# Expert groups of the two smallest counts in 32 places and four column tiles, in a two-layer mixture-of-experts trunk

## The chip, the cores and the metric

The kernel runs on one core of a Trainium2 chip, as one launch. The metric is the device time of that launch in microseconds (us), as the median of several runs. The engines are PE (TensorE matmul; its weight loads are listed as PEld), DVE (VectorE), ACT (ScalarE), POOL (GpSimd) and SP (SyncE, which here issues the weight transfers); 16 DMA engines move the data.

## What is computed

Two layers, each an attention-like mixer followed by a mixture of experts, over 512 tokens of width 1024. The change touches only the second half of a layer. Cut to that:

```python
def route(h, router_w, router_b):                     # 8 groups of 4 experts
    scores = jax.nn.sigmoid((h @ router_w).astype(jnp.float32))
    biased = scores + router_b.astype(jnp.float32)
    grp = biased.reshape(t, N_GROUPS, EXPERTS_PER_GROUP)
    group_score = jnp.sum(lax.top_k(grp, GROUP_SCORE_K)[0], axis=-1)
    g_sel = jnp.argmax(group_score, axis=-1)          # one group for each token
    in_group = (jnp.arange(N_EXPERTS) // EXPERTS_PER_GROUP)[None, :] == g_sel[:, None]
    _, idx = lax.top_k(jnp.where(in_group, biased, -jnp.inf), TOP_K)   # two experts of it
    w = jnp.take_along_axis(scores, idx, axis=-1)
    return idx, w / jnp.sum(w, axis=-1, keepdims=True)
...
    u = jax.nn.silu(xb @ w_gate[e]) * (xb @ w_up[e])  # 1024 -> 512
    y = (u @ w_down[e]) * gts[:, None]                # 512 -> 1024
...
    x = x + gt2 * y
```

A token goes to one group. With the reference's inputs the groups hold, sorted by count, 115, 96, 85, 71, 54, 46, 31 and 14 tokens in layer 0 and 108, 105, 94, 64, 50, 41, 30 and 20 in layer 1.

## The kernel before, in words

In each layer the kernel counts the tokens of each group, ranks the groups by count and gives each rank a fixed number of places: `CAPS` (line 31) is 128 for ranks 0 to 3 and 64 for ranks 4 to 7, 768 `PLACES` in all. A 0/1 matrix `Pt` gathers the normalized tokens into `hs`, whose columns are the places (L1370). All four experts of a group run on all places of the group; the gate weight of a place is zero where a token did not choose the expert. Tokens beyond a rank's places would be worked off by a loop behind `tc.If(nov > 0)` (L1686), which reads the group's weights again.

An expert is three matrices, each fetched as two transfers of 1 MB by SP (`fetch`, L1447) into one of eight raw buffers (tag `R8`: two in `ring`, four in `wm`, two in `late`). A transfer is issued as soon as the buffer's last user is done, so up to eight run ahead. Each transfer is used as two halves ("pieces"; `pieces` is asked for pieces up to four ahead of the one in use).

- A **wide** expert (rank 0 to 3) has each piece split into two parts by ACT and DVE (`split`) and runs three matmuls for each product (`three`): 24 matmuls of 512 columns for each of gate (`g`), up (`u`) and down (`y`).
- A **narrow** expert (rank 4 to 7) uses the raw fp32 weights as the moving operand and its 64 places as the stationary one; `halved` runs two matmuls side by side, one for each half of the columns, into the output partitions 0 to 63 and 64 to 127 (two column tiles). An fp32 matmul is two records in the trace.

`WHERE` (line 35) sets the order: **round** w (0 to 3) alternates the four experts of rank w with the four of rank w + 4; the last round ends with two wide experts and then two narrow ones. Within that order PE runs, for each expert e: gate of e + 1 (with the transposes of e, `turn`, in its midst), down of e, up of e + 1. When a group's fourth expert is done, its sum `ya` is multiplied with `gt2` and added back to the tokens (`combine`): it is cut into steps that are taken after each piece of the next experts. `combine_last` does the same for rank 7 at the end of the layer, with nothing beside it; in layer 0 it also makes the squares that the next layer's norm needs, in layer 1 it stores the result.

MoE-stage instructions of PE, DVE, ACT and POOL inside the expert loop keep their written order (`_Pinned`, whose line 122 stands in the trace for all of them). The next layer's first weights (`early`) are requested by SP right after the last expert's.

Of the kernel before, what the change touches and what calls it, by code (L numbers as in the profile page):

```python
# [139 lines left out]
def hybrid_trunk(ctx: ExitStack, tc: tile.TileContext, x, c, positions, w_mod, b_mod, norm1_g, norm2_g, w_in,  # L140
# [228 lines left out]
    for l in range(depth):  # L369
        first = l == 0  # L370
        with ExitStack() as ps:
# [919 lines left out]
            nth, rk, aw, cap, over, slot = [pt_([128, NT]) for _ in range(6)]  # L1291
# [4 lines left out]
            V.tensor_scalar(cap, rk, NWIDE - 0.5, CAPS[-1] - CAPS[0], op0=OP.is_gt, op1=OP.mult)  # L1296
            V.tensor_scalar(aw, rk, float(NWIDE), 0.0, op0=OP.subtract, op1=OP.max)
            V.tensor_scalar(cap, cap, float(CAPS[0]), None, op0=OP.add)
            V.scalar_tensor_tensor(aw, aw, CAPS[-1] / CAPS[0] - 1.0, rk, op0=OP.mult, op1=OP.add)
# [49 lines left out]
            def pre_done():  # L1349
# [7 lines left out]
                for n in range(2):  # L1357
                    A.dma_start(after["gt2h"][64 * n:64 * n + 64], bcast(mods[l, 5 * D + 512 * n:5 * D + 512 * n + 512], 512, 64))
# [134 lines left out]
            def up_part(src, e, gacc):  # L1493
                r, j = where[e]
                w = 512 if r < NWIDE else 256
# [5 lines left out]
                u_ = wm.tile([128, FE], tag="eu")[:, 0:w]  # L1501
                for q in range(w // 256):
# [5 lines left out]
            def turn(u_, e):  # L1508
# [7 lines left out]
                else:  # L1516
                    for k in range(2):
                        T.transpose(b[:, k], u_[:, k * 128:(k + 1) * 128], ident)
                    uT = wm.tile([128, 2, 128], tag="euT64")
                    A.copy(uT, b[:, 0:2])  # L1520
                return uT

            def down_part(src, e, uT, ya, amid=None):
                r, j = where[e]
                for k in range(4):
# [5 lines left out]
                    else:  # L1531
                        halved(ya[:, 0], uT[:, k % 2, 64 * (k // 2):64 * (k // 2) + 64], hl, 0, D, start, stop)
# [4 lines left out]
            def gain_y(ya, n, yf, wide_):  # L1537
                V.tensor_mul(yf, ya[:, n], after["gt2b"][:, n * 512:(n + 1) * 512] if wide_ else after["gt2h"])
                return yf

            def gated(ya, n, wide_):
                return parts(gain_y(ya, n, after["pool"].tile([128, 512], tag="eyf"), wide_))
# [253 lines left out]
```

## Time and profile before

| | us |
|---|---|
| median of 3 runs (1832.09 to 1835.33) | 1832.76 |
| the profiled execution | 1833.86 |
| its span, first to last instruction | 1832.1 |
| PE busy in the span | 1751.1 (96%) |
| DVE, ACT, POOL busy | 1113.6, 795.5, 88.9 |
| mean granted clock of PE | 0.98 of 2.4 GHz |
| read from HBM | 501.73 MB |

The span has two expert stages, one in each layer: about 449 to 964 us in layer 0 and 1312 to 1826 us in layer 1. In the rows, a busy share of PE says that a matmul was in flight, not that the array was full. "DMA share" is the mean busy share of the 16 DMA engines; where it is 1.0, they had a packet in hand all the time.

### The profile page before, as it was taken

What the parts mean: (1) busy time and instruction counts of PE and PEld (TensorE: products, weight loads), DVE (VectorE), ACT (ScalarE), POOL (GpSimd) and SP (SyncE); (2) the same over time, 40 slices, a digit from 0 to 9 for tenths busy, and PEclk for the clock granted to TensorE, in tenths of its full rate; (3) what the DMA queues carried; (4) which work ended last, traced back from release to release, by engine and by line L of the source; (5) the groups of instructions that cost most, each with busy time, mean ns of one, the idle gap of its engine ahead of it and who ended that gap; (6) DMA issues with size and microseconds to landing.
All of it is one profiled execution on the core that took longest, in us unless ns stands there. A gap on an engine that the chain in (4) does not pass through costs nothing. (4 is left out here: it accounts for less than half of the span.)

```text
span 1832.1 us, 28257 instructions
## 1 busy us (share of the span) xinstructions
PE 1751.1 (96%) x10891; PEld 1252.5 (68%) x10892; DVE 1113.6 (61%) x2004; ACT 795.5 (43%) x1215; POOL 88.9 (5%) x136
## 2 busy tenths in 40 slices
PE   5999999988999999999998999997999999999997
PEld 3866767777665666665748887986866666566673
DVE  4646564366548557566655778647555746756664
ACT  3344442354434443444523554445444344444450
POOL 1010000021000000000000110102000000000000
PEclk9999999998999999999998999998999999999998
DMA  9565547426999999999964211131899999999994
GB/s 329 159 220 181 176 154 227 161 97 267 368 421 374 396 422 365 413 422 355 423 249 141 70 47 47 47 131 47 322 381 421 364 411 422 360 414 416 360 421 180
DMA packets 115617, 512.11 MB, mean 280 GB/s; under 512 B 14978, under 2 KB 42896, under 8 KB 66320
## 3 DMA queue, kind: packets, MB, share of 16 engines
q1 hardware_dynamic: 111952, 504.93, 70.8%
q0 software_dynamic: 1072, 3.32, 0.5%
q10 hardware_dynamic: 2448, 1.94, 0.5%
q8 instruction: 89, 1.46, 0.3%
q14 instruction: 56, 0.46, 0.1%
HBM read 501.73 MB, written 8.42 MB: 278 GB/s over the span
## 5 line engine op out<-in xcount | busy, mean ns | idle before, releaser
L122 DVE TENSOR_TENSOR H<-R,H 128x1024 fp32r<-128x1024 f32 x368 | 431.2, 1219 | 97.6 <-ACT H L122 97.2
L122 ACT CAST H<-R 128x1024 fp32r<-128x1024 f32 x368 | 364.0, 1048 | 45.0 <-DMA R<-in_w_down_dram 27.5
L579 PEld LDWEIGHTS a<-H,u 128*128 128x128 f32 x1728 | 216.5, 190 | 45.0 <-issue 42.0
L579 PE MATMUL a<-H,u 128*128 128x256 f32 x1728 | 245.8, 291 | 0.0
L122 PE MATMUL y<-H,euT 128*128 128x512 f32 x768 | 188.6, 400 | 1.5 <-DVE euT L122 1.5
L122 PE MATMUL g<-H,exT 128*128 128x512 f32 x720 | 183.8, 402 | 0.0
L122 PE MATMUL u<-H,exT 128*128 128x512 f32 x720 | 177.0, 400 | 0.0
L122 PEld LDWEIGHTS y<-H,euT 128*128 128x128 f32 x768 | 141.6, 188 | 46.8 <-ACT H L122 9.2
L122 DVE SCALAR_TENSOR_TENSOR eu<-u,u,es 128x256 f32<-128x256 f32 x92 | 56.9, 672 | 191.5 <-PE u L122 191.5
L122 PEld LDWEIGHTS u<-H,exT 128*128 128x128 f32 x720 | 132.7, 188 | 54.1 <-issue 22.5
L122 PEld LDWEIGHTS g<-H,exT 128*128 128x128 f32 x720 | 131.4, 188 | 36.1 <-issue 8.5
L122 PE MATMUL g<-R,u 128*64 128x256 f32 x1024 | 126.9, 387 | 0.0
L122 PE MATMUL y<-R,euT 128*64 128x512 f32 x512 | 121.3, 602 | 1.1 <-ACT euT L122 1.1
L122 PE MATMUL u<-R,u 128*64 128x256 f32 x1024 | 118.9, 383 | 0.0
L122 DVE TENSOR_TENSOR u<-u,x 128x512 f32<-128x512 f32 x128 | 84.2, 682 | 45.7 <-PE x L122 45.5
L122 ACT COPY euT<-x 128x256 f32<-128x256 f32 x32 | 11.9, 372 | 211.8 <-PE x L122 191.2
L122 PEld LDWEIGHTS u<-R,u 128*64 128x64 f32 x1024 | 70.3, 137 | 45.2 <-issue 13.8
L122 PEld LDWEIGHTS g<-R,u 128*64 128x64 f32 x1024 | 67.0, 136 | 47.7 <-issue 20.6
L122 PE MATMUL x<-eyh,ePT 128*128 128x512 f32 (+1 forms) x256 | 75.5, 464 | 11.1 <-DVE u L122 7.5
L122 ACT CAST euT<-x 128x512 fp32r<-128x512 f32 x32 | 18.7, 584 | 151.5 <-PE x L122 151.5
L122 PEld LDWEIGHTS y<-R,euT 128*64 128x64 f32 x512 | 32.3, 136 | 63.7 <-issue 52.5
L122 PEld LDWEIGHTS x<-eyh,ePT 128*128 128x128 f32 (+1 forms) x256 | 34.0, 194 | 53.2 <-DVE u L122 33.0
(597 smaller groups left out, 2271.7 us busy)
## 6 DMA issues: line engine op xcount, KB each, us to landing
R<-in_w_gate_dram SPq DMA_DIRECT2D x128, 1024.0 KB
R<-in_w_up_dram SPq DMA_DIRECT2D x128, 1024.0 KB
R<-in_w_down_dram SPq DMA_DIRECT2D x128, 1024.0 KB
M<-in_w_mod_dram SPq DMA_DIRECT2D x80, 512.0 KB
R<-in_w_in_dram SPq DMA_DIRECT2D x20, 1024.0 KB
slab<-in_w_mod_dram SPq DMA_DIRECT2D x16, 512.0 KB
R<-in_w_in_dram SPq DMA_DIRECT2D x24, 256.0 KB
R<-in_w_out_dram SPq DMA_DIRECT2D x4, 1024.0 KB
```

The costliest lines, as they stand in the source:

```text
L122: return self.tc.keep_in_program_order(f(*args, **kw))
L579: T.matmul(acc[i // 2][:, i % 2], a[q][:, k, tk], hl[:, w, k], start=(i % 2 == 0 and q == 0 and k == 0 and n3 == 0), stop=(i % 2 == 1 and ...
```

## The change

Ranks 6 and 7 get 32 places instead of 64; ranks 0 to 5 keep theirs. `PLACES` becomes 736. For a rank of 32 places `halved` runs four matmuls side by side, each on a quarter of the columns, into the output partitions 0 to 31, 32 to 63, 64 to 95 and 96 to 127. For gate and up a quarter is every second column of one half (`wq`), so that one transposition instead of two turns the result. The sum `ya` of such a rank stands in 128 partitions by 256 columns; adding it back takes four quarter matmul groups for each of the four token tiles, in two rounds, instead of two half groups in one round. `gt2q` is a third copy of the output gain, loaded by four small transfers on ACT's queue. Two DVE instructions of 128x4 are added in the routing. The transfers of weights, their order, the buffers and the experts' order stay as they are.

```diff
-CAPS = (128,) * NWIDE + (64,) * (NG - NWIDE)
-OFFS = tuple(sum(CAPS[:r]) for r in range(NG))
-PLACES = sum(CAPS)
+CAPS = (128,) * NWIDE + (64,) * (NG - NWIDE - 2) + (32,) * 2
+OFFS = tuple(128 * min(r, NWIDE) + 64 * max(r - NWIDE, 0) for r in range(NG))
+PLACES = OFFS[-1] + CAPS[-1]
...
+            V.tensor_scalar(least, rk, NG - 2.5, CAPS[-1] - CAPS[NWIDE], op0=OP.is_gt, op1=OP.mult)
+            V.tensor_add(cap, cap, least)
...
-                for n in range(2):
-                    A.dma_start(after["gt2h"][64 * n:64 * n + 64], bcast(mods[l, 5 * D + 512 * n:5 * D + 512 * n + 512], 512, 64))
+                after["gt2q"] = wn.tile([128, 256])
+                for name, c in (("gt2h", 64), ("gt2q", 32)):
+                    w = D * c // 128
+                    for n in range(128 // c):
+                        o = 5 * D + w * n
+                        A.dma_start(after[name][c * n:c * (n + 1)], bcast(mods[l, o:o + w], w, c))
...
-            def halved(out, a, raw, c0, n, start, stop):
+            def halved(out, a, cap, columns, start, stop):
 
-                n //= 2
-                for h in range(2):
-                    T.matmul(out[64 * h:64 * h + 64, 0:n], a, raw[:, c0 + h * n:c0 + (h + 1) * n], start=start, stop=stop)
+                for h, w in enumerate(columns):
+                    T.matmul(out[cap * h:cap * (h + 1), 0:w.shape[-1]], a, w, start=start, stop=stop)
...
-                            halved(acc, hs[:, 2 * p + k, OFFS[r]:OFFS[r] + 64], hl, k * 512, 512, start, stop)
+                            w, cap = hl[:, k * 512:(k + 1) * 512], CAPS[r]
+                            wq = w.rearrange("p (q t k) -> p q k t", q=2, k=2)
+                            halved(acc, hs[:, 2 * p + k, OFFS[r]:OFFS[r] + cap], cap, [w[:, 0:256], w[:, 256:512]] if cap == 64 else
+                                   [wq[:, h // 2, h % 2] for h in range(4)], start, stop)
...
+                if w == 128:
+                    V.scalar_tensor_tensor(u_, acc[:, 0:w], gcs[:, r, j:j + 1], s, op0=OP.mult, op1=OP.mult)
...
-                        halved(ya[:, 0], uT[:, k % 2, 64 * (k // 2):64 * (k // 2) + 64], hl, 0, D, start, stop)
+                        cap, w = CAPS[r], D * CAPS[r] // 128
+                        a = uT[:, k % 2, 64 * (k // 2):64 * (k // 2) + 64] if cap == 64 else uT[:, 0, 32 * k:32 * k + 32]
+                        halved(ya[:, 0], a, cap, [hl[:, h * w:(h + 1) * w] for h in range(128 // cap)], start, stop)
...
-                if len(yhs) == 2:
+                w = min(512, D * cap // 128)
+                if cap == 128:
                     bs = [(n, pbank("x", 3), slice(0, 128), yhs[n]) for n in ns]
                 else:
-                    bs = [(n, pbank("x", 3), slice(64 * n, 64 * n + 64), yhs[0]) for n in ns]
+                    bs = [(n, pbank("x", 3)[:, 0:w], slice(cap * n, cap * n + cap), yhs[0]) for n in ns]
...
+            def rounds(r):
+
+                return {128: ((0,), (1,)), 64: ((0, 1),), 32: ((0, 2), (1, 3))}[CAPS[r]]
...
                 for i in range(NT):
-                    add(PT, yhs, (0, 1), i)
+                    for ns in rounds(r):
+                        add(PT, yhs, ns, i, CAPS[r])
```

On PE, in round 2 of layer 0, this stands between the up of a wide expert of rank 2 and the next one (`g`, `u`, `y` are gate, up and down; `R` is a raw buffer, `H` a split one; `eu` is transposed into `x`). Before:

```order
L122 MATMUL g_6687<-R_1241_6656,u_817_4391 64x256 x8
L122 MATMUL x_6704<-u_1_63,eu_6684 128x128 x4
L122 MATMUL g_6687<-R_1242_6670,u_817_4391 64x256 x8
L122 MATMUL y_6528<-H_1246_6690,euT_6709 128x512 x6
...
L122 MATMUL u_6758<-R_1253_6728,u_817_4391 64x256 x8
...
L122 MATMUL x_6808<-u_1_63,eu_6791 128x128 x2
...
L122 MATMUL y_1232_6628<-R_1265_6794,euT_1267_6811 64x512 x4
```

And now:

```order
L122 MATMUL g_6738<-R_1243_6707,u_818_4394 32x128 x16
L122 MATMUL x_6763<-u_1_63,eu_6735 128x128 x4
L122 MATMUL g_6738<-R_1244_6721,u_818_4394 32x128 x16
L122 MATMUL y_6556<-H_1248_6741,euT_6768 128x512 x6
...
L122 MATMUL u_6825<-R_1255_6795,u_818_4394 32x128 x16
...
L122 MATMUL x_6891<-u_1_63,eu_6874 128x128
...
L122 MATMUL y_1234_6671<-R_1267_6877,euT_1269_6893 32x256 x8
```

Nothing has changed places; each transfer of 1 MB is now used by twice as many matmuls of half the columns and half the outputs, and the narrow expert has one transpose instead of two.

On DVE, at the end of layer 0, `combine_last` stands between the last expert and the next layer's norm (`es` is the sum times the gain, `eyh` its split, `u_679` the tokens; L501 splits the next layer's early weights). Before:

```order
L122 TENSOR_TENSOR es_8123<-y_1403_7514,u_874_4751 128x512
L501 TENSOR_TENSOR H_1644_8638<-R_1537_8184,H_1644_8638 128x768
L122 TENSOR_TENSOR eyh_8125<-es_8123,eyh_8125 128x512
L501 TENSOR_TENSOR H_1647_8686<-R_1537_8184,H_1647_8686 128x768
L122 TENSOR_TENSOR u_679_3783<-u_679_3783,x_8128 128x512
L122 TENSOR_TENSOR u_679_3783<-u_679_3783,x_8129 128x512
...
L501 TENSOR_TENSOR H_1651_8738<-R_1538_8188,H_1651_8738 128x768
```

And now:

```order
L122 TENSOR_TENSOR es_8479<-y_1413_7745,u_876_4759 128x256
L122 TENSOR_TENSOR eyh_8481<-es_8479,eyh_8481 128x256
L122 TENSOR_TENSOR u_679_3783<-u_679_3783,x_8484 128x256
L122 TENSOR_TENSOR u_679_3783<-u_679_3783,x_8485 128x256
L501 TENSOR_TENSOR H_1662_9026<-R_1555_8572,H_1662_9026 128x768
L122 TENSOR_TENSOR u_679_3783<-u_679_3783,x_8492 128x256
L122 TENSOR_TENSOR u_679_3783<-u_679_3783,x_8493 128x256
L501 TENSOR_TENSOR H_1665_9074<-R_1555_8572,H_1665_9074 128x768
L122 TENSOR_TENSOR u_679_3783<-u_679_3783,x_8504 128x256
L122 TENSOR_TENSOR u_679_3783<-u_679_3783,x_8505 128x256
L501 TENSOR_TENSOR H_1669_9126<-R_1556_8576,H_1669_9126 128x768
```

The 8 additions of 512 columns have become 16 of 256; the early weights' splits stood before and behind the additions, and now all three stand among them.

## Rows read from the trace of the kernel before

**Rows 1.** The page's DMA issues: weight transfers of the experts, KB each.

```profile
R<-in_w_gate_dram SPq DMA_DIRECT2D x128, 1024.0 KB
```

**Rows 2.** Windows: us, busy PE PEld DVE ACT POOL, clock, DMA share, GB/s.

```profile
521.07:550.17 29.10, 29.10 (x159) 19.28 (x158) 16.36 (x16) 11.41 (x14) 0.00 (x0) 1.00 1.01 423
691.00:721.00 30.00, 28.73 (x140) 16.58 (x136) 23.27 (x34) 10.89 (x14) 0.00 (x0) 1.00 0.92 362
721.00:751.00 30.00, 30.00 (x164) 20.03 (x163) 17.52 (x18) 14.08 (x19) 0.00 (x0) 1.00 0.97 380
```

**Rows 3.** PE in order of time: start, us, matmuls; one undisturbed pair, then two starts.

```profile
521.07 1.95 PE L122 MATMUL g<-R,u 128*64 128x256 f32 x16
522.94 0.66 PE L122 MATMUL x<-u,eu 128*128 128x128 f32 x4
523.53 1.95 PE L122 MATMUL g<-R,u 128*64 128x256 f32 x16
525.41 5.84 PE L122 MATMUL y<-H,euT 128*128 128x512 f32 x24
531.17 3.67 PE L122 MATMUL u<-R,u 128*64 128x256 f32 x32
534.78 3.07 PE L122 MATMUL g<-H,exT 128*128 128x512 f32 x12
540.79 3.65 PE L122 MATMUL y<-R,euT 128*64 128x512 f32 x16
544.38 5.86 PE L122 MATMUL u<-H,exT 128*128 128x512 f32 x24
...
676.89 1.95 PE L122 MATMUL g<-R,u 128*64 128x256 f32 x16
745.39 1.95 PE L122 MATMUL g<-R,u 128*64 128x256 f32 x16
```

**Rows 4.** What SP's queue waited for: us in total, times, longest.

```profile
SPq L1447 <- PE g L122: 241.8, 60, 8.3
```

**Rows 5.** PE in order of time, elsewhere: matmuls of 32 outputs.

```profile
39.73 1.07 PE L322 MATMUL m<-slab,u 128*32 128x256 f32 x16
40.73 0.44 PE L452 MATMUL t<-u,P 128*128 128x128 f32 x2
...
119.97 0.62 PE L695 MATMUL l<-QF,KF 128*32 128x128 f32 x16
120.41 0.61 PE L322 MATMUL m<-M,u 128*32 128x256 f32 x8
```

**Rows 6.** Windows where the weight transfers end, layer 0 and layer 1.

```profile
938.00:939.00 1.00, 1.00 (x9) 0.48 (x8) 0.69 (x1) 0.00 (x0) 0.00 (x0) 1.00 0.20 82
1801.00:1802.00 1.00, 1.00 (x9) 0.49 (x8) 0.69 (x1) 0.00 (x0) 0.00 (x0) 1.00 0.16 66
```

**Rows 7.** PE in order of time: last downs of both layers, layer 1's first matmuls.

```profile
950.27 3.65 PE L122 MATMUL y<-R,euT 128*64 128x512 f32 x16 [0.53 <-ACT euT L122]
967.20 2.08 PE L450 MATMUL t<-at,u 128*128 128x128 f32 x8 [5.49 <-DVE at L429]
1813.28 3.65 PE L122 MATMUL y<-R,euT 128*64 128x512 f32 x16 [0.53 <-ACT euT L122]
```

**Rows 8.** Groups by form: busy us, mean ns of one, idle before.

```profile
L122 DVE TENSOR_TENSOR u<-u,x 128x512 f32<-128x512 f32 x128 | 84.2, 682 | 45.7 <-PE x L122 45.5
L902 DVE TENSOR_TENSOR p<-P,u 128x256 f32<-128x256 f32 x8 | 3.4, 423 | 0.4 <-ACT P L588 0.2
L1370 PE MATMUL x<-u,u 128*128 128x384 f32 x256 | 49.7, 357 | 7.1 <-DVE u L1310 6.5 <-ACT u L1376 0.6
L1297 DVE TENSOR_SCALAR u<-u 128x4 f32<-128x4 f32 x2 | 0.3, 164 | 0.0
```

**Rows 9.** Windows at the end of layer 0 and the start of layer 1.

```profile
956.00:960.00 4.00, 2.85 (x11) 1.49 (x11) 3.77 (x7) 2.96 (x9) 0.00 (x0) 0.88 0.44 132
972.00:976.00 4.00, 4.00 (x20) 4.00 (x20) 1.70 (x3) 0.78 (x1) 0.00 (x0) 0.50 0.90 283
```

More of the change, by code (lines that the diff above doesn't have):

```diff
@@ L1290, in hybrid_trunk @@
             tmp, tmp2 = pt_([128, NT, NG]), pt_([128, NT, NG])
-            nth, rk, aw, cap, over, slot = [pt_([128, NT]) for _ in range(6)]
+            nth, rk, aw, cap, over, slot, least = [pt_([128, NT]) for _ in range(7)]
             V.tensor_mul(tmp.rearrange("p i g -> p (i g)"), pc[:, 0:NT * NG], gf)
@@ L1494, in up_part @@
                 r, j = where[e]
-                w = 512 if r < NWIDE else 256
+                w = FE * CAPS[r] // 128
                 s = wm.tile([128, FE], tag="es")[:, 0:w]
@@ L1516, in turn @@
                 else:
-                    for k in range(2):
+                    n = CAPS[where[e][0]] // 32
+                    for k in range(n):
                         T.transpose(b[:, k], u_[:, k * 128:(k + 1) * 128], ident)
                     uT = wm.tile([128, 2, 128], tag="euT64")
-                    A.copy(uT, b[:, 0:2])
+                    A.copy(uT[:, 0:n], b[:, 0:n])
                 return uT
@@ L1535, in down_part, with gain_y, gated @@
                         amid()
[L1537 to L1542, printed above, removed]
+            def gain_y(ya, n, yf, r):
+                w = min(512, D * CAPS[r] // 128)
+                g_ = {128: "gt2b", 64: "gt2h", 32: "gt2q"}[CAPS[r]]
+                V.tensor_mul(yf[:, 0:w], ya[:, n, 0:w], after[g_][:, n * 512:n * 512 + w])
+                return yf[:, 0:w]
+            def gated(ya, n, r):
+                return parts(gain_y(ya, n, after["pool"].tile([128, 512], tag="eyf"), r))
             def parts(yf):
-                yh = after["pool"].tile([128, 2, 512], F32R, tag="eyh", bufs=2)
+                yh = after["pool"].tile([128, 2, 512], F32R, tag="eyh", bufs=2)[:, :, 0:yf.shape[-1]]
                 A.copy(yh[:, 0], yf)
@@ L1555, in squares, with add @@
                              accum_out=sums[:, i, n:n + 1])
-            def add(PT, yhs, ns, i):
-                if len(yhs) == 2:
+            def add(PT, yhs, ns, i, cap):
+                w = min(512, D * cap // 128)
+                if cap == 128:
                     bs = [(n, pbank("x", 3), slice(0, 128), yhs[n]) for n in ns]
                 else:
-                    bs = [(n, pbank("x", 3), slice(64 * n, 64 * n + 64), yhs[0]) for n in ns]
+                    bs = [(n, pbank("x", 3)[:, 0:w], slice(cap * n, cap * n + cap), yhs[0]) for n in ns]
                 for m in range(2):
@@ L1566, in add @@
                 for n, b, rows, yh in bs:
[L1567 removed]
+                    V.tensor_add(X[:, i, n * w:(n + 1) * w], X[:, i, n * w:(n + 1) * w], b)
+            def rounds(r):
+                return {128: ((0,), (1,)), 64: ((0, 1),), 32: ((0, 2), (1, 3))}[CAPS[r]]
             def combine_last(r, ya):
[L1571 removed]
                 if l + 1 < depth:
@@ L1574, in combine_last @@
                 PT = back(r)
-                yfs = [gain_y(ya, n, wm.tile([128, 512], tag=("es", "eu")[n]), wide_) for n in range(2 if wide_ else 1)]
+                yfs = [gain_y(ya, n, wm.tile([128, 512], tag=("es", "eu")[n]), r) for n in range(2 if r < NWIDE else 1)]
                 yhs = [parts(yf) for yf in yfs]
                 for i in range(NT):
-                    add(PT, yhs, (0, 1), i)
+                    for ns in rounds(r):
+                        add(PT, yhs, ns, i, CAPS[r])
                     if l + 1 < depth:
@@ L1592, in combine @@
                 for n in range(2 if r < NWIDE else 1):
-                    yhs.append(gated(ya, n, r < NWIDE))
+                    yhs.append(gated(ya, n, r))
                     yield
-                for ns in ((0,), (1,)) if r < NWIDE else ((0, 1),):
+                for ns in rounds(r):
                     for i in range(NT):
-                        add(PT, yhs, ns, i)
+                        add(PT, yhs, ns, i, CAPS[r])
                         yield
@@ L1750, in hybrid_trunk @@
                             for n in range(2):
-                                yf = gain_y(ya, n, wm.tile([128, 512], tag="es"), True)
+                                yf = gain_y(ya, n, wm.tile([128, 512], tag="es"), 0)
                                 for i in range(NT):
```

6 lines of the change are left out of this document (2 added, 4 removed).

## The prediction

> **What bounds the kernel now.** I read the windows of the expert stage first, then PE in order of time inside them, then what SP's queue waits for. One undisturbed pair, a narrow and a wide expert, takes 29.10 us, and PE is busy in all of it; in the same window the DMA engines have a share of 1.01 and move 423 GB/s [rows 2]. Both look full, so the reader has to see which of them sets the pace. A pair needs 12 transfers of 1024 KB [rows 1], 12.58 MB; used up in 29.10 us that is 432 GB/s, 2% more than the 423 that arrive. PE sets the pace, living on a store of up to eight buffers that shrinks by 0.7 us in each pair. The store is filled again where PE has something else to do: the pairs that begin at 676.89 end after 68.5 us instead of 58.2 [rows 3], 10.3 more, because the sums of the finished round are added back there. In those windows the DMA engines drop to 362 and 380 GB/s [rows 2], since SP finds no free buffer; over the whole span its longest wait is for PE's gate products, 241.8 us [rows 4]. So PE binds today, but transfers stand only 2% behind it. That is the point of this case: a faster PE runs into the transfers at once.
>
> **What the change takes from PE.** Today's narrow expert, start to start [rows 3]: gate 525.41 - 521.07 less the 0.59 of the wide expert's transposes (523.53 - 522.94) = 3.75; up 534.78 - 531.17 = 3.61; down 544.38 - 540.79 = 3.59; together 10.95 us. With 32 places, gate has 8 x 4 matmuls of 128 columns, 64 records, and so has up; down has 4 x 4 of 256 columns, 32 records. The trace has this shape elsewhere: 16 records of 32 outputs and 128 columns start within 120.41 - 119.97 = 0.44 us, 27.5 ns each, and 16 of 256 columns within 40.73 - 39.73 = 1.00 us, 62.5 ns each [rows 5]; four tiles do run side by side. That gives 1.76 + 1.76 + 2.00 = 5.5 us; I add 10% for switching shapes and take 6.1, a gain of 4.8 (bounds: 5.4 at the rows' pace; 0 if only two tiles overlap). What no row shows is a moving operand that takes every second fp32, as gate and up now do; its bounds are no cost and twice the time for these two, 7.0 + 2.2 = 9.2, and I take no cost, being nearest to [rows 5]. One transpose less and a shorter DVE product help where PE has slack anyway: nothing.
>
> **What remains of it.** A pair in rounds 2 and 3 then needs 29.1 - 4.8 = 24.3 us of PE, but its 12.58 MB at 423 GB/s need 29.7. The transfers become the bound, and 5.4 of PE time per pair turn into waits. The gain is therefore not 16 x 4.8 but what the DMA engines idle today in the second half of a layer, plus the store that PE still works off after the last transfer.
>
> Idle time of the transfers: at the start of round 2, 30 x (1 - 362/423) + 30 x (1 - 380/423) = 4.3 + 3.0 = 7.3 us [rows 2]; round 3 starts with the same pattern, another 7.3, and so in layer 1. In round 2 the store is full when the sums are added, so only PE's own saving in that pair comes back: 4.8. Before round 3 three pairs, each 5.4 short of data, have emptied the store; the 10.3 us of extra PE work now run while transfers fill it, and all 7.3 come back. Together 12.1 per layer (bounds 7.3, only one of them; 14.6, both).
>
> The end of a layer: today transfers end at 938.2 and 1801.2 [rows 6], while the last down ends at 950.27 + 3.65 = 953.9 and 1816.9 [rows 7]: 15.7 us of stored work. Afterwards the last four experts' narrow parts need less PE time than their transfers (four pieces of work of about 2 us, each behind 5 us of data), so PE has only the last transfer's half of a down left: 1.0 us, and I allow 1.3 for completion, 2.3 in all (bounds 1 and 5). Saved: 13.4 per layer.
>
> So the last down ends 12.1 + 13.4 = 25.5 us earlier in each layer.
>
> **What it adds.** The combine at the end has no cover. The additions: 16 x 0.423 instead of 8 x 0.682 [rows 8], +1.3; the gain product and its split on 256 columns give about 0.8 back; eight handovers from PE to DVE instead of four, at some 0.2 each, +0.8; in layer 0 one more split of early weights lies among the additions (768 columns, by the 0.682 for 512 about 1.0). I take +2.5 in layer 0 and +1.5 in layer 1 (bounds 0.5 and 6: the early weights are requested behind the last experts' transfers in SP's queue, and their splits stand in DVE's and ACT's order before later additions and squares, so if they come late, the next layer's norm waits). Combining rank 6 has the same 1.5 more on DVE, beside expert work: nothing. The gather L1370 shrinks from 384 to 368 columns, 4% of 49.7 us [rows 8], -2.1 in both layers; two more DVE steps (0.164 each [rows 8]) and four more tiny gate matmuls cost about 0.7 per layer, +1.4. The four small loads on ACT's queue fall in round 0, where transfers have their own slack soon after: nothing.
>
> **The sum.** 2 x 25.5 - 4.0 + 2.1 - 1.4 = 47.7 us. Against the profiled execution's 1833.86 that is 1786.2; that execution lies 1.1 above the median of 1832.76. I round to 1786 for the median. With all lower bounds a layer saves 7.3 + 10.7 - 6 = 12, with all upper ones 14.6 + 14.7 - 0.5 = 28.8: from 1809 to 1775.
>
> **The rivals.**
> - *The clock falls in the new waits.* PE now waits about 1.8 us three times in a pair. At the end of layer 0, with PE busy 2.85 of 4 us, the granted clock fell from 2.4 to 1.2 GHz (1.00 to 0.50; the mean there is 0.88), and 972 to 976 ran at 0.50 with PE busy all the time [rows 9]. A fall in front of each wide block would cost at least 2 us (4 us of work at half speed), 6 per pair, just over the slack of 5.4; then PE is the bound again by 0.6 us x 8, round 3's 7.3 don't come back, and the end runs at half speed, about +3: 15 per layer, 1816. Against it: the waits lie between blocks of 6 us in which PE is dense, and once PE falls behind, the waits close. [...]
> - *Strided columns cost double.* Gate and up 7.0, down 2.2: the narrow expert gains 1.7 instead of 4.8. A pair is 27.4, still under 29.7, but the store empties only by 2.3 per pair, 6.9 before round 3, whose extra work is 10.3 - 1.7: of the idle time 1.7 + 5 come back, at the end nothing, less the added 2, some 5 per layer: 1824.
> - *The transfers have no limit at 423.* Then PE keeps the pace and all 16 x 4.8 = 77 come: 1757. Against it: 423 at a share of 1.01 while PE uses up 432. [...] The row's 423 decides.
> - *Slower: the four tiles don't overlap.* It would show in PE's records of gate, up and down. At today's pace of 3.61/32 = 113 ns per record of 256 columns in two overlapping tiles, one tile alone at a time would take 64 x 113 = 7.2 for gate and for up and 32 x 226 = 7.2 for down, 21.7: 10.7 more per narrow expert, 16 x 10.7 = 171, about 2008. It decides from 57 ns per record of 128 columns upwards, where the narrow expert costs what it does now. Against it stand the 27.5 ns of [rows 5].
> - *The change doesn't do what it says, since a group has over 32 tokens.* Then the loop behind L1686 reads that group again: 24 x 1.05 MB, 60 us each at 423 GB/s. The routing of the reference's inputs gives 31 and 30 for rank 6, one place to spare.
>
> **How the numbers follow.** Forecast 0.69, the clock 0.13, strided columns 0.06, no limit 0.05, no overlap (or two tiles at a time, about 1836) 0.05, overflow 0.02. The range reaches from 1774, just past the upper bounds, to 1816, the clock, and leaves out half of the clock's rival, the strided one and those below. A measurement can tell about 0.2%, 3.7 us, from no change. Faster are the first four, 0.93; 0.01 within; slower 0.06.
>
> **What would show it.** Records of `g` and `u` with 128x128 at about 28 ns each; windows of rounds 2 and 3 all at 422 to 423 GB/s from the first pair of round 2 on, with PE busy near 82% and waiting for DMA of `R`; SP's waits for PE gone there; the last down 2 to 3 us behind the last transfer; the combine longer by 1 to 3 us. I am wrong if the transfers still drop at the start of round 3, if the clock leaves 1.00 in the stage, if narrow experts take over 9 us, or if the last down trails the transfers by over 6 us.

## The result, and the profile after

The changed kernel takes 1811.76 us (median of 5 runs, 1808.69 to 1814.11) against 1832.76: a ratio of 0.9882, 95% interval 0.9868 to 0.9897. It is faster by 21 us; forecast were 47. The profiled execution took 1812.13 us, its span is 1810.2 us and the mean granted clock 0.97.

The mechanics of the change came as forecast. PE in order of time in the changed kernel (start, us, matmuls, in brackets the wait ahead and what ended it), one narrow expert of 32 places and its neighbours, which answers to [rows 3]:

```profile
728.97 2.06 PE L122 MATMUL u<-R,u 128*32 128x128 f32 x64
730.96 3.07 PE L122 MATMUL g<-H,exT 128*128 128x512 f32 x12
...
736.85 1.93 PE L122 MATMUL y<-R,euT 128*32 128x256 f32 x32
738.71 5.82 PE L122 MATMUL u<-H,exT 128*128 128x512 f32 x24
744.46 1.14 PE L122 MATMUL g<-R,u 128*32 128x128 f32 x32
```

Up takes 730.96 - 728.97 = 1.99 us and down 738.71 - 736.85 = 1.86. So the four tiles run side by side, and every second column as moving operand costs little at most: 64 records in 1.99 us are 31 ns each, against 27.5 in [rows 5]. The ends of the two layers, same view, answering to [rows 7]:

```profile
938.78 1.07 PE L122 MATMUL y<-R,euT 128*32 128x256 f32 x16 [0.33 <-DMA R<-in_w_down_dram]
...
956.15 1.23 PE L450 MATMUL t<-at,u 128*128 128x128 f32 x4 [5.28 <-DVE at L429]
...
1792.31 1.07 PE L122 MATMUL y<-R,euT 128*32 128x256 f32 x16 [0.80 <-DMA R<-in_w_down_dram]
```

The last matmuls of a layer now wait for the last transfer, no longer the other way round. What did not come is that this transfer lands earlier. Three differences make up each layer (landings are the completions of the weight transfers in the trace; layer 1 is counted from its first matmul at L450):

| after less before, us | forecast | layer 0 | layer 1 |
|---|---|---|---|
| last weight transfer lands | -12.1 | 938.74 - 940.00 = -1.3 | (1792.27 - 956.15) - (1802.49 - 967.20) = +0.8 |
| from there to the end of the last down | -13.4 | 1.1 - 13.9 = -12.8 | 1.1 - 14.4 = -13.3 |
| from there to the next layer's first matmul, or the span's end | +2.5, +1.5 | 16.3 - 13.3 = +3.0 | 16.8 - 15.1 = +1.7 |
| sum | | -11.1 | -10.8 |

The whole shortfall stands in the first line. Windows of 30 us show where (us, busy PE PEld DVE ACT POOL, clock, DMA share, GB/s): first the kernel before, then the changed one, answering to [rows 2].

```profile
810.00:840.00 30.00, 29.71 (x141) 18.44 (x139) 22.01 (x29) 12.30 (x15) 0.00 (x0) 1.00 1.00 404
840.00:870.00 30.00, 29.03 (x160) 18.54 (x159) 19.66 (x22) 13.19 (x16) 0.00 (x0) 1.00 0.88 338
```

```profile
720.00:750.00 30.00, 29.37 (x284) 21.55 (x282) 20.30 (x23) 15.65 (x20) 0.00 (x0) 0.95 0.97 386
750.00:780.00 30.00, 27.94 (x254) 21.03 (x253) 17.00 (x17) 13.41 (x16) 0.00 (x0) 1.00 1.01 421
780.00:810.00 30.00, 25.36 (x232) 18.02 (x232) 17.19 (x17) 14.46 (x17) 0.00 (x0) 0.94 1.01 421
810.00:840.00 30.00, 25.62 (x214) 16.98 (x212) 21.51 (x32) 11.99 (x15) 0.00 (x0) 1.00 1.01 420
840.00:870.00 30.00, 28.78 (x224) 20.59 (x224) 18.52 (x26) 13.28 (x16) 0.00 (x0) 0.89 0.86 342
```

From 750 to 840 us the transfers are the bound, as forecast, and PE has time to spare (25.4 of 30 us busy). Yet from 840 on they stand still as much as before, 342 GB/s against 338. And the granted clock leaves 1.00, which it did nowhere in the rounds of the kernel before (1.00 from 426.6 to 959.0 us and from 1286.8 to 1819.2).

Two things worked out from the trace carry the rest of the text. **The store** is the time from a transfer's landing to the first matmul that uses it; at 18 to 19 us (18.0 and 18.7 at transfer 152 below) all eight buffers are taken and the next transfer has to wait. **Idle transfers** are the parts above 2.5 us of those gaps between two landings (1024 KB each) that are longer than 2.75 us, summed over quarters of a layer's 192 transfers, which nearly are the four rounds. Where two runs have the same code, such a sum differs by up to about 2 us (18.7 in the changed kernel and 20.6 in e2, first quarter of layer 1).

| store in layer 0, us, at transfer | 118 | 126 | 134 | 142 (round 3) | 147 | 152 | 160 |
|---|---|---|---|---|---|---|---|
| before | 8.6 | 8.3 | 7.5 | 8.1 | 13.0 | 18.0 | 11.8 |
| after | 4.9 | 2.6 | 1.2 | 6.2 | 10.4 | 18.7 | 9.6 |

The store runs down to 1.2 us, as it should, and some 60 us later it is full again. That is the puzzle which the experiments take up: PE, though its narrow experts are faster, takes 854.5 - 803.4 = 51 us from transfer 138 to transfer 152, and took 853.1 - 807.9 = 45 before.

### The profile page after: what moved, and what is told of

It reads as the page before. It is cut to its first block, busy times and chain, and to the rows that moved or that the text cites. A ratio compares the mean times of both kernels' runs of the same rounds, so it can differ in the third digit from the quotient of the medians.

```text
span 1810.2 us, 30985 instructions
## 1 busy us (share of the span) xinstructions
PE 1695.9 (94%) x12235; PEld 1248.8 (69%) x12236; DVE 1107.3 (61%) x2040; ACT 793.7 (44%) x1215; POOL 88.3 (5%) x136
## 5 line engine op out<-in xcount | busy, mean ns | idle before, releaser
L122 ACT CAST H<-R 128x1024 fp32r<-128x1024 f32 x368 | 365.1, 1048 | 109.5 <-DMA R<-in_w_down_dram 44.2
L122 PEld LDWEIGHTS u<-H,exT 128*128 128x128 f32 x720 | 132.5, 188 | 49.9 <-issue 14.9
L122 DVE SCALAR_TENSOR_TENSOR eu<-u,u,es 128x256 f32<-128x256 f32 (+1 forms) x92 | 51.7, 615 | 138.0 <-PE u L122 138.0
L122 DVE TENSOR_TENSOR u<-u,x 128x512 f32<-128x512 f32 (+1 forms) x160 | 87.4, 575 | 45.6 <-PE x L122 45.6
L122 PE MATMUL x<-eyh,ePT 32*128 32x256 f32 (+2 forms) x320 | 85.7, 443 | 19.9 <-DVE u L122 12.9
L122 PE MATMUL g<-R,u 128*32 128x128 f32 (+1 forms) x1536 | 103.4, 324 | 0.0
L122 PE MATMUL y<-R,euT 128*32 128x256 f32 (+1 forms) x768 | 94.1, 457 | 2.0 <-DMA R<-in_w_down_dram 1.1
L122 PE MATMUL u<-R,u 128*32 128x128 f32 (+1 forms) x1536 | 92.8, 313 | 0.0
L122 PEld LDWEIGHTS g<-R,u 128*32 128x32 f32 (+1 forms) x1536 | 61.6, 121 | 35.0 <-issue 18.9
L122 PEld LDWEIGHTS x<-eyh,ePT 32*128 32x128 f32 (+2 forms) x320 | 43.3, 210 | 59.5 <-DVE u L122 30.6
L122 PEld LDWEIGHTS u<-R,u 128*32 128x32 f32 (+1 forms) x1536 | 63.2, 118 | 29.7 <-issue 13.5
L122 ACT COPY euT<-x 128x256 f32<-128x256 f32 (+1 forms) x32 | 10.2, 319 | 159.3 <-PE x L122 145.5
L122 ACT CAST euT<-x 128x512 fp32r<-128x512 f32 x32 | 18.7, 584 | 113.1 <-PE x L122 113.1
L545 ACT CAST H<-R 128x1024 fp32r<-128x1024 f32 x40 | 41.9, 1047 | 56.3 <-PE a L579 37.7
```

What stands on the lines that cost most here:

```text
L122: return self.tc.keep_in_program_order(f(*args, **kw))
L545: A.copy(hl[:, 0], raw[:, 4 * q:4 * q + 4])
```

## The experiments

All times are medians; each ratio is to the kernel before on the same chip, with its 95% interval.

| run | edit of the changed kernel | us | ratio |
|---|---|---|---|
| e1 | only rank 7 at 32 places | 1812.92 | 0.9889 (0.9874 to 0.9904) |
| e2 | look-ahead 2 from round 2 on | 1802.05 | 0.9832 (0.9819 to 0.9845) |
| e3 | small gain table copied | 1805.70 | 0.9855 (0.9840 to 0.9870) |
| e4 | narrow order 6, 4, 5, 7 | 1807.39 | 0.9865 (0.9850 to 0.9880) |
| e5 | e2 and e3 | 1794.75 | 0.9787 (0.9774 to 0.9800) |
| e6 | kernel before, look-ahead 2 | 1845.59 | 1.0066 (1.0053 to 1.0080) |
| e7 | kernel before, four more loads | 1838.61 | 1.0039 (1.0025 to 1.0053) |
| e8 | order 6, 4, 5, 7, look-ahead 2 all through, e3 | 1804.88 | 0.9845 (0.9832 to 0.9858) |
| f1 | e3, look-ahead 3 from round 2 on | 1799.63 | 0.9813 (0.9800 to 0.9827) |
| f2 | e3, look-ahead 2 from later in round 2 on | 1793.97 | 0.9786 (0.9773 to 0.9799) |
| f3 | e3, only rank 7 at 32 places | 1804.13 | 0.9839 (0.9826 to 0.9853) |
| g1 | e3, matmuls that fill PE's waits | 1811.73 | 0.9877 (0.9860 to 0.9894) |
| g2 | e3, look-ahead 1 from round 2 on | 1810.67 | 0.9876 (0.9861 to 0.9891) |
| g3 | f2, table for 64 places copied too | 1793.84 | 0.9784 (0.9770 to 0.9797) |
| h1 | small loads ahead of the large one | 1805.74 | 0.9855 (0.9838 to 0.9873) |

### What is rank 6 worth, and what does the look-ahead cost

Theory A: ACT and DVE work in their written order, and in it the splits of wide weights stand up to four pieces ahead of PE's use. Four pieces are 2 MB, 5 us of transfers at the 421 GB/s of the windows above. Once the store is under 5 us, a split waits for weights that have not landed, and what PE needs now stands behind it. The trace of the changed kernel shows it at the end of rank 2. PE, then ACT and DVE in order of time:

```profile
804.94 6.81 PE L122 MATMUL y<-H,euT 128*128 128x512 f32 x22 [0.84 <-DVE euT L122]
811.68 2.06 PE L122 MATMUL u<-R,u 128*32 128x128 f32 x64
816.16 0.51 PE L122 MATMUL x<-eyh,ePT 128*128 128x512 f32 x1 [2.42 <-ACT eyh L122]
...
822.69 0.33 PE L122 MATMUL x<-u,eu 128*128 128x128 f32 x1 [1.59 <-DVE eu L122]
```

```profile
811.01 2.00 ACT L122 CAST H<-R 128x1024 fp32r<-128x1024 f32 x2 [5.25 <-DMA R<-in_w_gate_dram]
815.49 0.62 ACT L122 CAST eyh<-eyf 128x512 fp32r<-128x512 f32 x1 [2.48 <-DVE eyf L122]
```

```profile
812.10 1.23 DVE L122 TENSOR_TENSOR H<-R,H 128x1024 fp32r<-128x1024 f32 x1 [4.95 <-ACT H L122]
813.24 0.48 DVE L122 TENSOR_SCALAR ePT<-u,u 128x512 fp32r<-128x512 f32 x1
813.63 1.22 DVE L122 TENSOR_TENSOR H<-R,H 128x1024 fp32r<-128x1024 f32 x1
814.77 0.69 DVE L122 TENSOR_TENSOR eyf<-y,u 128x512 f32<-128x512 f32 x1
```

The down sums of rank 2 are complete at 811.75. DVE has been idle for 4.95 us, but first it has to finish two splits whose data landed only at 810.99; the gain product `eyf` starts at 814.77, 3 us late, and PE stands 2.42 us for `eyh`. Nothing that PE waits for here is a weight.

**e1: only rank 7 at 32 places** (rank 6 back to 64; the count's threshold goes with it).

```
-CAPS = (128,) * NWIDE + (64,) * (NG - NWIDE - 2) + (32,) * 2
+CAPS = (128,) * NWIDE + (64,) * (NG - NWIDE - 1) + (32,)
-V.tensor_scalar(least, rk, NG - 2.5, ...)
+V.tensor_scalar(least, rk, NG - 1.5, ...)
```

> Only the last rank (7, round 3) gets 32 places; rank 6 (round 2) keeps 64. Theory A (round 2's saving is eaten by waits of PE for ACT and DVE, which stand behind weights that have not landed): narrowing rank 6 bought nothing, the whole gain is round 3's, which works off the store of buffers by the layer's end. Time within 4 us of the changed kernel's 1811.8: 1808 to 1816. Rival B (round 2's saving does reach the end, 5 to 7 us per layer, and something else that the change adds took 10 us back): 1821 to 1828. In the trace, A: no wait of PE over 1.5 us for euT or eyh between 690 and 840 us, no clock fall there, last transfer of layer 0 at 939 to 941 us.

Measured 1812.92, the same as with both ranks. Rank 6's faster experts, half of the edit, buy nothing in the changed kernel; the gain is rank 7's, which works off the store by the layer's end. No wait for `euT` or `eyh` over 0.3 us stands between 690 and 840. That fits theory A but does not prove it.

**e2: a shorter look-ahead**, two pieces instead of four from round 2 on.

```
-src = _Ahead(pieces(items), lambda: 4)
+ahead = [4]
+src = _Ahead(pieces(items), lambda: ahead[0])
 for e in range(ne):
+    if e == 15:
+        ahead[0] = 2
```

> The changed kernel, but from round 2 on ACT and DVE split weights only two half-transfers ahead of PE instead of four. Theory A: a store of 1.2 to 3 us no longer puts ACT's in-order queue behind data that have not landed; PE's waits for euT, eu, eyh between 770 and 846 us (about 10 us in sum) fall below 5, the clock falls at 719, 805 and 842 us go or shrink, the store at the start of round 3 stays under 15 us instead of 18.7, and a layer gains 3 to 6 us: 1799 to 1806. Rival C (the time is lost in round 3's own start, in the sums of the finished groups, whatever ACT does): no change, 1810 to 1814. Rival D: the splits come too late and PE waits for H: slower, 1815 to 1830.

1802.05: 9.7 us gained, with not one matmul changed. The idle transfers of the last quarter fall from 6.0 and 7.6 us (layers 0 and 1) to 1.3 and 1.7, the other quarters do not fall. The store at transfer 152 is 13.1 instead of 18.7 us.

**e6: the control**, the same edit on the kernel before.

> The kernel before with the same shorter look-ahead from round 2 on, as a control. Theory A: its store never falls under 7 us in rounds 2 and 3, so ACT never stands behind data there, and the look-ahead is worth nothing: 1831 to 1835. Rival F (a shorter look-ahead is simply a better order of ACT and DVE, whatever the store): 1822 to 1828.

Slower by 13 us. So the shorter look-ahead is not simply a better order; by itself it is worse. A part of that is splits that come late: PE's waits for `H` between 683 and 867 us, of which the kernel before has none, are now (us in total, times, longest)

```profile
PE y L122 <- DVE H L122: 2.9, 5, 0.6
...
PE g L122 <- DVE H L122: 0.7, 1, 0.7
```

All waits of PE in this stretch grew by 3.8 us, of the 6.5 that a layer lost; the rest was not followed. The shorter look-ahead pays only where the store runs dry. My expectation of no change was wrong: the sign rules out rival F, but theory A had not foreseen the loss.

**f1 and g2: three pieces and one**, with the copied gain table of e3 (four: 1805.70, two: 1794.75).

> As e5 (gain table copied), but splits three half-transfers ahead from round 2 on instead of two. ACT then stands behind data when the store is under about 3.8 us instead of 2.5 (two) or 5 (four). If the loss at round 3's start grows with the look-ahead step by step, the time lies between e5's 1794.8 and e3's 1805.7, near 1800, with 3 to 4 us of idle transfers in the last quarter of a layer. If depth two loses as much to late splits as it wins (PE waits for H, seen in e6): three is the best of both, 1788 to 1793.

> As e5 with only one half-transfer split ahead from round 2 on (four gave 1805.7, three 1799.6, two 1794.8). If ACT behind data is all that counts: 1790 to 1794. If late splits now make PE wait for H before each piece: 1798 to 1815, with PE's waits for H several times e5's 8 us in 690 to 860.

Four, three, two, one pieces: 1805.7, 1799.6, 1794.8, 1810.7 us. Down to two each piece is worth 5 to 6 us; with one, PE waits for `H` everywhere, 15 us in sum from 683 to 867 (10 in e5), and the granted clock falls for 6.8 us at 812:

```profile
PE g L122 <- DVE H L122: 4.3, 6, 0.8
PE y L122 <- DVE H L122: 3.7, 6, 0.8
PE u L122 <- DVE H L122: 3.1, 5, 0.9
PE y L122 <- ACT H L122: 2.3, 4, 0.6
```

**f3: rank 7 alone, with the copied table.**

> Only rank 7 at 32 places, gain table copied, look-ahead four: against e5 it tells what rank 6's 32 places are worth once nothing else is lost. If the two cures only remove losses that rank 6's faster experts bring on themselves: 1806 to 1808 (1812.9 less the 6.1 of the loads), so rank 6 is worth about 12 us with the shorter look-ahead, and about 1 to 2 without (e3, 1805.7). If the loads cost nothing here: 1812.

1804.13. With a look-ahead of four, rank 6's 32 places bring nothing (e3, 1805.70, is 1.6 us slower, and the intervals overlap); e5, below, with its look-ahead of two is 9.4 us faster than f3, 4.7 per layer. So rank 6's 32 places do pay once the look-ahead is short. Rank 7 alone with a look-ahead of two was not run, so the 9.4 us belong to the two edits together.

### The four small loads

The first quarter of a layer had 1.0 and 1.8 us more of idle transfers after the change (18.4 and 18.7 against 17.4 and 16.9), though rounds 0 and 1 run the same code. ACT and then PE at that place in the changed kernel:

```profile
466.39 8.94 ACTq L122 DMA_DIRECT2D u<-u  x7
475.38 0.38 ACT L122 ACTIVATE es<-g 128x256 f32<-128x256 f32 x1 [8.00 <-DMA u<-u]
```

```profile
476.75 0.50 PE L122 MATMUL g<-H,exT 128*128 128x512 f32 x1 [0.70 <-ACT H L122]
478.01 2.83 PE L122 MATMUL g<-H,exT 128*128 128x512 f32 x11 [0.76 <-DVE H L122]
481.99 0.44 PE L122 MATMUL x<-u,eu 128*128 128x128 f32 x2 [1.15 <-DVE eu L122]
```

ACT is held for 8 us among its own DMA issues, and PE loses 2.6 us behind it.

**e3: the 32-place table copied from the full one** by GpSimd, without the four loads.

```
-for name, c in (("gt2h", 64), ("gt2q", 32)):
-    ...
-        A.dma_start(after[name][c * n:c * (n + 1)], bcast(mods[l, o:o + w], w, c))
+for n in range(2):
+    A.dma_start(after["gt2h"][64 * n:64 * n + 64], ...)
+for n in range(4):
+    rows = slice(32 * n, 32 * n + 32)
+    nc.gpsimd.tensor_copy(after["gt2q"][rows], after["gt2b"][rows, 256 * n:256 * n + 256])
```

> The changed kernel, but the 32-place gain table is copied out of the full one by GpSimd instead of by four small loads on ACT's queue. If these loads delay ACT and with it rounds 0 and 1 (transfers of layer 0 up to round 2 took 2.6 us more than before, layer 1's 1.0): item 94 of layer 0 lands 1 to 2.6 us earlier (683.3 to 685), time 1807 to 1811. If they are hidden, as forecast, or if the store is full at round 2's start anyway: 1811 to 1813.

1805.70, 6.1 us gained, more than expected: the first quarter's idle transfers fall to 14.9 and 16.6. The three issues that are left:

```profile
466.81 1.69 ACTq L122 DMA_DIRECT2D u<-u  x3
468.54 0.39 ACT L122 ACTIVATE es<-g 128x256 f32<-128x256 f32 x1 [0.74 <-DVE H L122]
```

**e7: the four loads alone**, added to the kernel before into a table that nothing reads.

```
+unused = wn.tile([128, 256])
+for n in range(4):
+    o = 5 * D + 256 * n
+    A.dma_start(unused[32 * n:32 * n + 32], bcast(mods[l, o:o + 256], 256, 32))
```

> The kernel before with four more loads of 32 x 256 on ACT's queue at the place where the changed kernel has them, into a table that nothing reads. If issuing them holds ACT for about 7 us in round 0 (8.94 us for seven issues against 1.68 for three) and PE waits 2.6 us for it: 2 to 3 us per layer, 1836 to 1839, with PE busy about 12.4 of the 15 us from 470 to 485. If the full store before round 2 takes it up: 1832 to 1834.

1838.61, 6 us slower, but from 1833.89 to 1842.06: the cost varies from execution to execution. The profiled one is the 1833.89: there ACT is held 4.91 us and PE does not wait. So PE had cover for 4.91 us of this here and not for the 8.00 in the changed kernel.

**h1: the same seven loads in another order.** Of the seven issues six are out by 469.73 and the last starts at 475.02, as the changed kernel's ACT queue shows in two windows:

```profile
467.60 2.13 ACTq L122 DMA_DIRECT2D u<-u  x4
...
475.02 0.31 ACTq L122 DMA_DIRECT2D u<-u  x1
```

In the trace's operands the seventh carries the same semaphore as the first, a load of 512 KB (number 110 in both), and its record waits for that semaphore. The first load's last part landed at 475.00 us, 0.02 before the seventh starts; in layer 1 it is 1327.33 and 1327.35.

```
-A.dma_start(after["gt2b"], bcast(mods[l, 5 * D:6 * D], D))
-for name, c in (("gt2h", 64), ("gt2q", 32)):
+for name, c in (("gt2q", 32), ("gt2h", 64)):
     ...
+A.dma_start(after["gt2b"], bcast(mods[l, 5 * D:6 * D], D))
```

> The changed kernel with the same seven loads on ACT's queue in another order: the four of 32 KB first, then the two of 128 KB, the one of 512 KB last. In the changed kernel six are issued by 469.7 us and the seventh only at 475.0; it carries the semaphore of the first, the 512 KB one, which may have to land first. If the seventh waits for the first load's landing: with a small load first the seventh goes out within 1 to 3 us, PE's 2.6 us of waits at 476 to 482 go, and the time is that of the copied table, 1804 to 1808. If the number of issues or the bytes hold ACT: unchanged, 1810 to 1814.

1805.74, just e3's time, with all seven loads. Seven issues now take 3.84 us, and PE has no wait there:

```profile
464.93 3.84 ACTq L122 DMA_DIRECT2D u<-u  x7
468.82 0.38 ACT L122 ACTIVATE es<-g 128x256 f32<-128x256 f32 x1 [2.90 <-DMA u<-u]
```

Here the first load landed at 468.40 and the seventh starts at 468.43. So neither the bytes nor the number of issues cost the 6 us: ACT waited for the first load to land before it could issue the seventh.

### Both cures, and two that failed

**e5: look-ahead two and the copied table.**

> The changed kernel with both edits: splits two half-transfers ahead from round 2 on, and the 32-place gain table copied by GpSimd. If the two losses are separate (four DMA issues on ACT's queue in round 0, ACT and DVE waiting behind weights around the start of round 3), the gains of 6.1 and 9.7 us add: 1796, within 1794 to 1799. If they are the same time counted twice (what round 0 gives back is lost again at a full store before round 2): 1801 to 1803. In the trace: idle transfers about 15 us in the first quarter of a layer as before the change, 1 to 2 us in the last.

1794.75, 17 us under the changed kernel: the gains add (6.1 + 9.7 = 15.8). Each has its own quarter:

| idle transfers by quarter, us | layer 0 | layer 1 |
|---|---|---|
| before | 17.4, 7.7, 7.3, 7.6 | 16.9, 9.1, 7.1, 7.5 |
| after | 18.4, 8.3, 5.6, 6.0 | 18.7, 8.1, 5.7, 7.6 |
| e3, table copied | 14.9, 8.5, 5.4, 6.1 | 16.6, 8.0, 6.4, 8.0 |
| e2, look-ahead two | 17.9, 9.0, 6.1, 1.3 | 20.6, 8.1, 5.8, 1.7 |
| e5, both | 15.4, 8.7, 5.8, 1.6 | 17.3, 7.5, 6.5, 1.8 |

Windows of e5 over the start of round 3 (columns as above); the second answers to the 342 GB/s of the changed kernel:

```profile
810.00:840.00 30.00, 26.03 (x198) 16.04 (x190) 23.61 (x37) 12.37 (x16) 0.00 (x0) 1.00 1.01 422
840.00:870.00 30.00, 28.58 (x259) 21.01 (x260) 20.88 (x27) 14.74 (x20) 0.00 (x0) 1.00 0.99 406
```

**f2 and g3: two refinements**, the look-ahead shortened two pairs later, and then the 64-place table copied as well.

> As e5, but the look-ahead falls from four to two only with the third narrow expert of round 2 instead of the first. While the store is full at round 2's start the longer look-ahead is the better one (e6: two costs 6 to 7 us per layer there), so PE's waits for H at 690 to 750 us (about 3 us) should go: 1 to 3 us per layer, 1789 to 1793. If those waits lie under transfers that stand still anyway: 1794 to 1796.

> As f2 (look-ahead two from round 2's third narrow expert on), with the table for 64 places copied by GpSimd too, so that ACT issues one load at that place instead of three (1.68 us for three in the kernel before). Layer gain 0.5 to 1.2 us if round 0 still has PE behind ACT there: 1791 to 1793. If three issues are hidden: 1793 to 1795.

1793.97 and 1793.84: no difference from e5 that these runs can tell. All three beat the kernel before by 2.1 to 2.2% and the changed one by 1%.

**e4 and e8: the 32-place groups in rounds 0 and 3.**

```
+BESIDE = (6, 4, 5, 7)
-WHERE = [(r, j) for w in range(NWIDE) for j in range(4) for r in (w, w + NWIDE)]
+WHERE = [(r, j) for w in range(NWIDE) for j in range(4) for r in (w, BESIDE[w])]
```

> The changed kernel, but the narrow groups go beside the wide ones in the order 6, 4, 5, 7 instead of 4, 5, 6, 7: the two groups of 32 places lie in rounds 0 and 3, not in 2 and 3. Theory A: in round 0 the buffers are full and PE is behind (17 to 18 us of idle transfers in the first quarter of a layer), so a faster PE there gives time back, and before round 3 the store does not run empty, so no waits for ACT. Transfers of round 0 end 5 to 10 us earlier, the sums at the start of round 1 refill the store, and a layer gains 4 to 8 us over the changed kernel: 1796 to 1804. Rival C (what PE saves ahead of a round's start is always given back at that start): 1810 to 1814. Rival E (rounds 1 and 2 fall back to PE's pace with a full store and the end trails as before): 1812 to 1820.

> All three edits: narrow groups in the order 6, 4, 5, 7, splits two half-transfers ahead all through, gain table copied. If PE's saving in round 0 refills nothing but idle transfers at the start of round 1 (there 7 to 8 us of idle now, 1 to 2 expected), and rounds 1 and 2 run the store from about 10 us up to full only by round 3: idle transfers fall by 3 to 6 us per layer against e5, 1784 to 1790. If the idle time only moves from round 1's start to round 3's: 1793 to 1798.

e4 is 4.4 us under the changed kernel, between the two expectations. With both cures the order loses 10 us against e5, more than either expectation: round 1's start gets its idle time down (3.8 and 2.3 us in the second quarter), but the third and fourth quarters rise to 10.5 and 8.2 (layer 1: 10.5 and 9.1). e8 also has the look-ahead of two in the rounds with a full store, where e6 found it harmful; how much of the 10 us is that, these runs do not separate.

**g1: is it the clock?** In the changed kernel the granted clock fell after the waits. Three windows: two falls, and the stretch ahead of the second one, with PE busy 4.63 of 6 us:

```profile
804.90:808.20 3.30, 3.26 (x8) 2.59 (x9) 2.25 (x2) 0.87 (x2) 0.00 (x0) 0.50 1.01 420
842.40:849.20 6.80, 6.80 (x48) 4.34 (x40) 5.18 (x10) 4.58 (x6) 0.00 (x0) 0.50 1.00 390
836.00:842.00 6.00, 4.63 (x53) 3.06 (x54) 4.72 (x10) 0.90 (x1) 0.00 (x0) 1.00 1.01 408
```

What it costs can be read off the same work at a granted clock of 1.00 and of 0.50 (the traces give the clock as this share, none in GHz), PE in order of time:

```profile
838.88 0.66 PE L122 MATMUL g<-R,u 128*32 128x128 f32 x16
...
844.07 1.08 PE L122 MATMUL g<-R,u 128*32 128x128 f32 x16
...
846.25 2.93 PE L122 MATMUL y<-H,euT 128*128 128x512 f32 x6
...
849.57 1.64 PE L122 MATMUL y<-H,euT 128*128 128x512 f32 x6
```

With the like rows between them the fall at 842 costs about 3.2 us, the one at 805 some 1.5 (22 down matmuls in 6.81 us; 24 take 5.84 in [rows 3]): 4.7 of PE time. The waits of PE from 800 to 860 grew from 1.6 us before to 8.0. Together that is 11 us lost while the store filled. g1 put 47 small matmuls where PE waits, to hold the clock and keep the waits:

```
+def filler(n):
+    b = pbank("x", 3)
+    for _ in range(n):
+        T.matmul(b[:, 0:128], ident, ident, start=True, stop=True)
```

> As e3 (gain table copied, look-ahead four), with 47 matmuls of the identity by itself (128 columns, about 0.17 us each, 7.8 us in sum per layer) into banks that nothing reads, put where PE waits for ACT and DVE in the changed kernel's trace: at the downs of the third and fourth wide expert of round 2 (773, 803 us), at two transposes (787, 822) and at the first additions of ranks 2 and 6 (816, 841). Waits stay, since ACT and DVE do what they did; only the clock can change. If the falls of the clock (10.2 us at half speed around round 3's start) are what costs: no fall there, idle transfers of the last quarter 6 down to 2 to 3, 1797 to 1801. If the waits themselves cost the time: 1804 to 1807, falls gone. If the added matmuls don't fit into the waits: over 1807.

1811.73 (1804.66 to 1813.16), 6 us slower than e3: the third outcome, the added matmuls do not fit into the waits. Of e3's falls in layer 0, at 717, 802 and 840 us, the first two are gone; the third came at 838 and another at 848. The idle transfers of the last quarter rose from 6.1 and 8.0 us to 12.3 and 9.3. So this run does not separate clock and waits.

The traces of the other runs separate them better. The store fills between PE's first use of transfer 138 and that of transfer 152, and PE does the same work there in the following runs (309 to 313 matmul records). Windows over that stretch (columns as above): the changed kernel in layers 0 and 1, then e2 in both, then layer 0 of f2 and of g3, which have the same code there.

```profile
803.40:854.50 51.10, 44.66 (x309) 30.27 (x309) 36.42 (x54) 20.89 (x26) 0.00 (x0) 0.90 0.97 397
1655.70:1707.20 51.50, 46.65 (x310) 31.31 (x310) 36.50 (x54) 20.83 (x26) 0.00 (x0) 0.87 0.96 394
```

```profile
802.50:848.90 46.40, 41.38 (x313) 27.37 (x314) 37.08 (x54) 21.71 (x27) 0.00 (x0) 1.00 1.01 422
1652.90:1698.90 46.00, 41.15 (x311) 27.36 (x311) 37.09 (x54) 21.54 (x27) 0.00 (x0) 1.00 1.01 418
```

```profile
799.90:846.20 46.30, 41.37 (x309) 27.35 (x309) 37.02 (x54) 21.71 (x27) 0.00 (x0) 1.00 1.01 422
799.20:847.10 47.90, 42.89 (x312) 28.32 (x312) 37.55 (x54) 21.76 (x27) 0.00 (x0) 0.96 1.01 422
```

PE is idle for 6.4 and 4.9 us in the changed kernel and for 5.0 and 4.9 in e2. The shorter look-ahead thus takes away 1.4 us of waiting in one layer and none in the other; it turns a few long waits, up to 2.42 us, into many of at most 0.8 and one of 1.3. The other 3.3 and 5.5 us are PE's busy time, the same work at a mean clock of 1.00 instead of 0.90 and 0.87. f2 and g3 agree: idle 4.9 and 5.0 us, yet g3 takes 1.6 us longer at a clock of 0.96.

So what e2 gave back at round 3's start, 4.7 and 5.5 us, was for the larger part the clock. With a look-ahead of four and both ranks at 32 places (the changed kernel, e3, g1, h1) the clock fell in all eight such stretches, for 3.4 to 13.7 us; with two (e2, e5, f2, g3) in two of eight, for 3.4 us each. With one (g2) it fell in both. So in these runs the clock fell there more often with four than with two; why it falls behind one wait and not behind another like it, these runs do not show.

## Why the prediction was wrong, step by step

- **PE sets the pace, transfers 2% behind:** right. Freed of 5 us per pair, PE ran into the transfers at once, 419 to 422 GB/s at a share of 1.01 over whole windows.
- **A narrow expert in 6.1 us:** right, 2.11 + 1.99 + 1.86 = 6.0 us without the transposes (gate is 745.52 - 744.46 and 747.30 - 746.25 in the same view). The 10% for switching shapes was an estimate that no row shows. Strided columns came nowhere near twice the time: up's 31 ns a record are 13% over the 27.5 of [rows 5], which may have other grounds.
- **The store at a layer's end, -13.4:** right, -12.8 and -13.3. This is the gain that was measured. The 1.3 us for completion were an estimate that no row shows; with the down itself, 1.1 passed from the last landing to its end.
- **The combine, +2.5 and +1.5:** right, +3.0 and +1.7. The 0.2 us for a handover were an estimate too.
- **Idle transfers coming back, -12.1 per layer:** this is the step that failed. Its lower bound was 7.3, and the last landing moved by -1.3 and +0.8. It has two terms.
  - *Round 2, "PE's own saving in that pair comes back: 4.8".* Measured 1.7 and 1.4 (7.3 to 5.6, 7.1 to 5.7), and with both cures 1.5 and 0.6. While the store is full, a transfer starts when a buffer comes free (SP's longest wait in the changed kernel is still for PE's gate products, 211.0 us over the span), so the idle time follows the work that PE does then. By the landings most of it falls from 716 to 728 us before and from 718 to 730 after (4.5 and 4.1 us), while rank 6's first up runs at 729 and its down at 737 (rows above). Only its gate, 2 us less, came in time. I had taken the whole expert. No run tests this reading.
  - *Round 3, "all 7.3 come back".* Measured 1.6 and none. The premise held: the store was empty before round 3. What failed is the overlap: the 10.3 us of extra work were to run at PE's old pace while transfers fill the store, but PE took 51 us from transfer 138 to 152 instead of 45. What I left out is what an empty store does to the engines between: ACT and DVE stand behind weights that are not there, PE waits for them (idle 6.4 and 4.9 us instead of 1.5), and the clock falls (3.3 and 5.5 us against e2). With both cures, 6.0 and 5.7 came back.
- **"The four small loads: nothing":** wrong, 6 us in all, by h1 ACT's wait for the first load to land: the seventh issue, with the same semaphore, starts 0.02 us behind that landing. I had looked at their bytes and at transfers, not at the engine that issues them.
- **The sum.** Missing were 46.8 - 21.0 = 25.8 us. The loads are 6, the look-ahead about 10, round 2's term 2 x 3.2 = 6.4 by the idle times. The gather was to give 2.1 and gave 0.5: 256 matmuls of 368 columns take 357 ns each as those of 384 did, 49.2 us against 49.7. The layers' ends and the combine fell short by 1.4. Less than 1 is left, within the noise.
- **The rivals.** "The clock falls in the new waits" came nearest: it named 1816, falls in the new waits and round 3's idle time not coming back. At round 3's start it is most of what happened, 3.3 and 5.5 us of the 4.7 and 5.5 that e2 got back. But it had PE wait for data and the clock fall ahead of each wide block. The waits were for ACT and DVE, the falls were few, and the store did run empty before round 3. The clock fell three times in rounds 2 and 3 of layer 0, for 3.4 to 6.8 us each, and in e5 once, for 3.4, so not at every wait. The other rivals did not occur.
- **Of the listed signs**, two that were to prove me wrong showed: the transfers dropped at round 3's start, and the clock left 1.00.

## What to carry to other kernels

When a change turns a compute-bound stretch into a transfer-bound one, look at every engine that prepares data ahead in a fixed order: how far ahead it works, in us of transfers, against the store that will be left. Here ACT and DVE worked 5 us ahead against a store of 1.2 us, and urgent small work stood behind data that had not landed: 2.42 us of PE's wait for `eyh`. The engine that was freed had waits to spare as long as the transfers bound (PE busy 25.4 of 30 us at 421 GB/s); it needed its full pace again where the buffers refilled, and just there it was at half its clock for 10.2 of 51 us. Look at the granted clock of that stretch, not only at its waits. And by the reading of round 2, which no run tests, time that is freed while all buffers are full comes back only if it lies ahead of the release that the next transfer waits for.

## What the runs showed of the hardware that was not expected

- ACT's DMA issues are cheap one by one (0.31 to 0.59 us each in layer 0 of the changed kernel), but the seventh in a row started 5.3 us after the sixth was out and 0.02 us after the first, a 512 KB load with the same semaphore, had landed. With a 32 KB load first, the same seven took 3.84 us instead of 8.94.
- With PE busy 4.63 of 6 us, in waits of 1.4 us and less, the granted clock went from 1.00 to 0.50 for 6.8 us, although PE was busy in all of these 6.8. The like wait at the same place in the code was 1.28 us in f2, where the clock held, and 1.29 in g3, where it fell for 3.4 us: the same code, in two executions.
